# Two-step modulation blocks, more raw weight places and late matrix reads in a two-layer hybrid step

## The chip, the cores and the metric

The kernel runs on one core of a Trainium2 chip. The metric is the device time of one execution in microseconds (us), the median of several runs. One profiled execution of the kernel before is shown beside them; all rows of the trace are of that one.

## What is computed

The reference is one inference step of a hybrid backbone of two layers, in fp32. 128 prompt tokens and 256 sample tokens of width 1024 go through the same weights. Cut to what matters here:

```python
def layer(x, mod, p, lam_init, ctx, angs):
    sh1, sc1, g1, sh2, sc2, g2 = jnp.split(mod, N_MOD, axis=-1)
    h = rmsnorm(x, p['norm1_g']) * (1.0 + sc1) + sh1
    mix, st = token_mixers(h, p, lam_init, ctx, angs)   # four head groups, one of them an SSM
    x = x + g1 * mix
    h = rmsnorm(x, p['norm2_g']) * (1.0 + sc2) + sh2
    return x + g2 * sq_relu_mlp(h, p), st

def sq_relu_mlp(h, p):
    a = jax.nn.relu(h @ p['mlp_w1'])                    # 1024 x 4096
    return (a * a) @ p['mlp_w2']                        # 4096 x 1024

def adaln(cond, p):                                     # the modulation: 6 vectors of 1024
    return jax.nn.silu(cond) @ p['w_ada'] + p['b_ada']  # 1024 x 6144
```

The SSM part of `token_mixers` is not scanned step by step in the kernel: matrices that stand for the scan are built from its parameters and used in matmuls. One set of them is wanted for each layer.

## The kernel before

The 384 tokens are three tiles of 128. The work runs in five stages, which follow each other with some overlap: start, mix 0, MLP 0, mix 1, MLP 1. "mix" is normalization, the input projection, the four head groups and the output projection of a layer.

**Weights.** A matrix product in fp32 precision is made of three matmuls on a high and a low half of each operand (`mm3`). `stream` (line 833) fetches the weights in the order of a list: SP issues the DMA of one raw weight (512 KB) into a raw place ("wr"), ACT copies its high half and DVE subtracts the low half into a split place ("ws"), and the raw place is free again. Raw weights of the modulation (names ad1...) are not split: they stay in their raw place until PE has used them. `phase` (line 596) adds places to the base of three ws and four wr: in MLP 0 `CF["mlp"]` adds 3 ws, 4 small working tiles ("tk") and 2 wr.

**The MLP.** `mlp` (line 2223) walks through 16 pairs fp of two blocks i. `h1_block(fp, i)` makes 24 matmuls of 128x384 into a PSUM tile h with the two w1 halves of the pair (names w1, layer, pair, half: w10140 is layer 0, pair 14, half 0). ACT takes the relu to rl, DVE squares it, ACT copies the high half aT and DVE makes the low half. `w2_mm` then adds 18 matmuls of 128x512 into mo with one w2 weight per block (w2025 is layer 0, block 25). The h block of a pair stands one pair ahead of its mo.

**What else runs in MLP 0.** The modulation of layer 1 (`ada_split`, line 777) is done there, in 24 steps: three thirds of eight k. A step takes two raw weights (ad1hk0 and ad1hk1 for third h and step k) and is four column-tiled matmuls, which the trace shows as 8 records on 32 columns of the array; after each third come the transposes adat. `CF["adafp"]` says at which pairs steps are made, `CF["adan"]` how many behind each w2, `CF["adak"]` how many stand in one block. The SSM matrices of layer 1 are prepared there too (`ssm_tables`, and `ssm_ahead` with `ssm_prep`, on DVE and ACT in an area called arena): a quarter's matrices are written to DRAM by POOL (`WE<-arena`, 1.1 MB, four times) and its taps by ACT (`KD<-kb`). In mix 1 they are read back by `ssm_load` (line 1355) into tiles we and TT, by POOL's queue, two quarters at a time. The first two quarters' tiles have their room in MLP 0 already, so POOL issues those four reads in MLP 0.

**What sets the order.** Every operation is recorded by a helper (so all have line L366 in the trace), and a planner (`arrange`, line 423) orders each engine's operations by a due time to which the table `SHIFT` adds an offset for the kind of the tile that is written (`kind`, line 93: letters and one digit, mostly the layer). Manual dependencies then fix each engine's order. The engines and the DMA queues issue strictly in that order.

Of the kernel before, what the change touches and what calls it, by code (L numbers as in the profile page):

```python
# [20 lines left out]
L = 2  # L21
NT = 3

CF = {"order": "dba", "adafp": [2,3,4,5,6,7,8,9,10,11,12,13], "adan": 1, "psc": "VV", "qW": "Q", "adasplit": 0, "lq": 1, "KO": [3, 2, 1, 0], "adaat": 1, "kt": [["KTm", 1], ["QTm", 1], ["KTd", 1], ["QTd", 1]], "fair": 0, "adaf": 0, "eng": {"pT1": "A", "KTd": "A"}, "mlag": 4, "glag": 4, "NTK": 13, "W": 4, "prep": 0.0, "chain": 0.0, "tails": 0.0, "tailm": 0.0, "mla": 0.0, "gqa": 0.0, "diff": 0.0, "ada": 0.0,
      "stream": 0.0, "tab": 0.0, "main": 0.0, "tab1": 30.0, "rot": 10.0, "adak": 1, "balance": 0, "xbt": [2, 4], "xoff": 3.0, "woff": 5.0, "modoff": 0.0, "ahead": 0.0, "aheadoff": 0.0, "rotoff": [40.0, 0.0], "taboff": 10.0, "xlag": 5.0, "epool": 0, "lowp": [], "rotp": [], "hlp": [],"xat": 9, "st0": 20.0, "xs": 4, "mlp": [[3, 4, 2], [4, 4, 4]], "np": 2, "n1": 1, "tm": 1, "lnlag": 0.0, "dlag": 0.0, "hb1need": ["mla"], "dneed": ["mla"], "opneed": ["diff0"], "w1m": 1, "lnb": [400, 300, 0], "cache": 0.0}
CFS = [{**CF, **CF.get(f"L{l}", {})} for l in range(2)]
NTK = CF["NTK"]
KO = tuple(CF["KO"])
if CF["order"] == "dba":
# [9 lines left out]
WEIGH = (0,)  # L39

SHIFT = {
# [24 lines left out]
    "out_new_diff_k_dram": -75.4, "out_new_diff_v_dram": 130.1, "out_new_gqa_k_dram": -5.5,  # L66
    "out_new_gqa_v_dram": -67.1, "out_new_mla_ckv_dram": 55.9, "out_new_mla_krope_dram": -124.5,
    "out_new_ssm_im_dram": 170.2, "out_new_ssm_re_dram": -36.4, "out_y_prompt_dram": 17.1,
# [21 lines left out]
    "zred": 25.0,}  # L90


def kind(n):

    m = re.match(r"([A-Za-z_]+)(\d?)", n)
    return m[1] + m[2]


# [435 lines left out]
def hybrid_step(ctx: ExitStack, tc: tile.TileContext, I, O, plan=None):  # L534
# [29 lines left out]
    def lo(shape, name, tag=None, bufs=1, dt=F32):  # L564
        return alloc("lo", shape, name, tag, bufs, dt)
# [782 lines left out]
    def ssm_taps(l, qt, eng=None):  # L1348
        kd = KD[l][qt]
        TT = lo([128, 4, 128], f"TT{l}{qt}", "TT", 2)  # L1350
        (eng or DK).dma_start(TT, bass.AP(tensor=kd.tensor, offset=kd.offset,
                                ap=[[16, 8], [960, 16], [240, 4], [1, 128]]))
        return TT

    def ssm_load(l, qt, out):

        we = lo([128, 2176], f"we{l}{qt}", "we", 2)
        P.dma_start(we, WE[l][:, qt])
        W = [we[:, d * 576:(d + 1) * 576].rearrange("p (g j c) -> p g j c", g=4, j=9) for d in range(2)]
        out[qt] = (W, we[:, 1152:2176].rearrange("p (d g s) -> p d g s", d=2, g=4), ssm_taps(l, qt, P))  # L1360
        yield
# [930 lines left out]
            rl = tk([128, 384], f"rl{l}{fp}{i}")  # L2292
            act(rl, ps[:, 0:384], AF.Relu)
            tt(rl, rl, rl, OP.mult)
            act(aT_[:, i, 0], rl, AF.Copy)
            tt(aT_[:, i, 1], rl, aT_[:, i, 0].bitcast(F32), OP.subtract)
            done(rl, ps)
# [288 lines left out]
```

## Time and profile before

| | us |
|---|---|
| runs | 1084.15, 1086.51, 1090.27 |
| median | 1086.51 |
| profiled execution | 1094.41 |
| its span | 1092.6 |
| PE busy in the span | 1017.6 |
| DVE, ACT, POOL busy | 704.9, 489.7, 71.6 |
| start (0 to 62), mix 0 (62 to 276) | 62, 214 |
| MLP 0 (276 to 604) | 328 |
| mix 1 (604 to 808) | 204 |
| MLP 1 (808 to 1085) | 277 |

The stages are cut where the first or last matmul of their kind stands in the trace. 198.68 MB pass the DMA engines in the span, 182 GB/s in the mean. To read it: PE's share says which engine bounds the whole; a stage's table says where PE is not busy; the list of waits says for whom; the timeline of the engine that it waited for says what that engine was doing.

### The profile page before, as it was taken

The page shows a single profiled execution, that of the slowest core. Times are in us where ns is not written, and L with a number is a line of the kernel's source. Part 1 is how long each engine was busy: PE and PEld are TensorE (multiplying, and loading weights), DVE is VectorE, ACT ScalarE, POOL GpSimd, SP SyncE. Part 2 cuts the span into 40 slices and gives each one's busy share as a digit, 9 for nine tenths or more (in the row PEclk, how much of TensorE's full clock was granted, in tenths as well). Part 3 has the DMA queues.
Part 4 walks back from the last instruction along what each step waited for, and adds up shares of the span by engine and source line. Part 5 has one row for each costly group of instructions (what it writes and reads, how often), then busy time and mean ns, then how long its engine had stood idle before and what let it go on. Part 6 is the DMA issues. An engine that isn't in the chain of part 4 may idle for free. (4 is left out here: it accounts for less than half of the span.)

```text
span 1092.6 us, 16805 instructions
## 1 busy us (share of the span) xinstructions
PE 1017.6 (93%) x6156; PEld 814.9 (75%) x6156; DVE 704.9 (65%) x1706; ACT 489.7 (45%) x1056; POOL 71.6 (7%) x140
## 2 busy tenths in 40 slices
PE   6599989999899899999799999998989999999996
PEld 1476746657898678788678787676779999999995
DVE  8988987767798745644235767988685433444345
ACT  2653447754642334324233543588555333433332
POOL 0021200002000000000000012000200000000001
PEclk9899999999899999999899999998999999999999
DMA  9674584558447776788974446500673334444202
GB/s 362 227 272 140 176 263 167 172 178 279 153 142 254 273 260 209 241 280 280 292 243 155 134 134 194 174 16 21 223 259 97 123 125 138 135 154 149 83 20 77
DMA packets 103812, 198.68 MB, mean 182 GB/s; under 512 B 11937, under 2 KB 60577, under 8 KB 102449
## 3 DMA queue, kind: packets, MB, share of 16 engines
q1 hardware_dynamic: 86192, 164.76, 46.0%
q10 hardware_dynamic: 15232, 16.85, 4.9%
q0 software_dynamic: 2304, 16.00, 4.3%
q8 instruction: 48, 0.79, 0.3%
q14 instruction: 36, 0.29, 0.1%
HBM read 175.22 MB, written 19.07 MB: 178 GB/s over the span
## 5 line engine op out<-in xcount | busy, mean ns | idle before, releaser
L366 PE MATMUL mo<-w,aT 128*128 128x512 f32 x1152 | 347.3, 395 | 0.0
L366 PE MATMUL h<-HT,w 128*128 128x384 f32 x1344 | 315.4, 341 | 13.7 <-ACT rl L366 7.3
L366 PEld LDWEIGHTS h<-HT,w 128*128 128x128 f32 x1344 | 245.4, 190 | 26.7 <-ACT rl L366 8.4
L366 PEld LDWEIGHTS mo<-w,aT 128*128 128x128 f32 x1152 | 213.9, 188 | 47.2 <-issue 9.5
L366 DVE TENSOR_TENSOR rl<-rl 128x384 f32<-128x384 f32 (+1 forms) x62 | 35.2, 569 | 110.2 <-ACT rl L366 110.2
L366 ACT ACTIVATE rl<-h 128x384 f32<-128x384 f32 x56 | 27.2, 486 | 153.9 <-PE h L366 143.3
L366 PE MATMUL op<-wo,HT 128*128 128x512 f32 x288 | 74.6, 406 | 2.7 <-DVE rseb L366 1.5
L366 PEld LDWEIGHTS op<-wo,HT 128*128 128x128 f32 x288 | 52.8, 190 | 15.1 <-DVE wo L366 3.9
L366 PE MATMUL ada<-adaw,sil 128*2 128x512 f32 (+1 forms) x192 | 35.6, 612 | 12.8 <-DVE rsaa L366 8.4
L366 PE MATMUL h1t<-w,HT 128*128 128x256 f32 x288 | 40.2, 299 | 6.5 <-ACT HT L366 6.3
L366 PEld LDWEIGHTS h1t<-w,HT 128*128 128x128 f32 x288 | 37.9, 205 | 7.8 <-ACT HT L366 7.2
L366 ACT ACTIVATE aT<-rl 128x384 fp32r<-128x384 f32 x56 | 29.3, 523 | 31.0 <-DVE rl L366 31.0
L366 DVE TENSOR_TENSOR aT<-rl,aT 128x384 fp32r<-128x384 f32 x56 | 31.1, 555 | 17.7 <-ACT aT L366 17.7
L366 POOL TENSOR_TENSOR x<-x,res 128x512 f32<-128x512 f32 x10 | 14.7, 1488 | 367.0 <-DVE res L366 348.0
L366 ACT ACTIVATE pd<-sd,nmxd 128x384 f32<-128x384 f32 (+1 forms) x48 | 24.3, 514 | 7.3 <-DVE nmxd L366 5.3
L366 PEld LDWEIGHTS ada<-adaw,sil 128*2 128x2 f32 (+1 forms) x192 | 3.9, 87 | 31.5 <-DMA adaw<-in_w_ada_dram 18.5
L366 PE MATMUL ip0c<-wi0c,HT 128*128 128x512 f32 x72 | 19.8, 427 | 7.6 <-ACT HT L366 7.4
L366 DVE TENSOR_REDUCE nmxd<-sd 128x1 f32<-128x384 f32 (+1 forms) x40 | 20.5, 524 | 5.4 <-PE sd L366 5.1
L366 PEld LDWEIGHTS ip0c<-wi0c,HT 128*128 128x128 f32 x72 | 14.0, 202 | 11.7 <-ACT HT L366 8.3
L366 PE MATMUL ip1b<-wi1b,HT 128*128 128x512 f32 x72 | 21.3, 427 | 0.0
L366 PE MATMUL ip0b<-wi0b,HT 128*128 128x512 f32 x72 | 21.2, 424 | 0.0
L366 PE MATMUL ip1a<-wi1a,HT 128*128 128x512 f32 x72 | 20.7, 418 | 0.0
(824 smaller groups left out, 1883.9 us busy)
## 6 DMA issues: line engine op xcount, KB each, us to landing
adaw<-in_w_ada_dram SPq DMA_DIRECT2D x48, 512.0 KB, 5.1
x<-x SPq DMA_DIRECT2D x36, 256.0 KB, 2.6
S<-ph POOLq DMA_DIRECT2D x2, 2400.0 KB, 8.5
phr<-S ACTq DMA_DIRECT2D x8, 600.0 KB, 5.6
WE<-arena POOLq DMA_DIRECT2D x4, 1088.0 KB, 5.6
we<-WE POOLq DMA_DIRECT2D x4, 1088.0 KB, 10.2
gate<-gate ACTq DMA_DIRECT2D x16, 256.0 KB, 5.9
x<-in_x_sample_dram SPq DMA_DIRECT2D x8, 256.0 KB, 6.3
```

Source lines behind the costliest of these rows:

```text
L366: r_ = f(*args, **kw)
```

## The change

1. Two modulation steps stand in one block (`adak` 2), and a block is made behind both w2 weights of every second pair (3, 5, ..., 13) in place of one step behind each w2 of the pairs 2 to 13. The list of weights has four modulation weights behind each w2 of those pairs.
2. MLP 0 has 8 raw places in place of 6, 5 split places in place of 6, and one working tile less.
3. A one-column tile `late` is copied by POOL from rl of block (13,1) of layer 0. Before POOL issues a read of we or TT it copies `late` into the first column of the tile that is to be read into; the read overwrites it.
4. All offsets in `SHIFT` are new. `kind` first takes a suffix like `_1` off a name.

The diff, with two rows of the table:

```diff
-CF = {..., "adafp": [2,3,4,5,6,7,8,9,10,11,12,13], "adan": 1, ..., "adak": 1, ..., "mlp": [[3, 4, 2], [4, 4, 4]], ...}
+CF = {..., "adafp": [3,5,7,9,11,13], "adan": 2, ..., "adak": 2, ..., "mlp": [[2,3,4],[4,4,4]], ...}
 SHIFT = {
-    "E0": -16.3, "E2": -15.4, "ET0": -39.7, "HT": 0.8, "Hc0": -102.9, ...
+    "E0": -42.8, "E2": -24.7, "ET0": -55.7, "HT": -9.6, "Hc0": -136.1, ...
...
 def kind(n):
-    m = re.match(r"([A-Za-z_]+)(\d?)", n)
+    m = re.match(r"([A-Za-z_]+)(\d?)", re.sub(r"_\d+$", "", n))
     return m[1] + m[2]
...
     def ssm_taps(l, qt, eng=None):
         kd = KD[l][qt]
         TT = lo([128, 4, 128], f"TT{l}{qt}", "TT", 2)
+        if eng is not None:
+            P.tensor_copy(TT[:, 0, 0:1], lcs["late"])
         (eng or DK).dma_start(TT, ...)
...
     def ssm_load(l, qt, out):
         we = lo([128, 2176], f"we{l}{qt}", "we", 2)
+        P.tensor_copy(we[:, 0:1], lcs["late"])
         P.dma_start(we, WE[l][:, qt])
...
             rl = tk([128, 384], f"rl{l}{fp}{i}")
             act(rl, ps[:, 0:384], AF.Relu)
             tt(rl, rl, rl, OP.mult)
+            if l + 1 < L and (fp, i) == (13, 1):
+                lcs["late"] = ct([128, 1], "late")
+                P.tensor_copy(lcs["late"], rl[:, 0:1])
             act(aT_[:, i, 0], rl, AF.Copy)
```

**POOL's queue, from the last write of the SSM matrices to the end of MLP 0.** WE and KD are the matrices and taps in DRAM, we10 and TT10 the tiles of layer 1's quarter 0, x100 a residual. Before:

```order
L366 DMA WE_1_88<-arena1_4466 128x2176 x4
L366 DMA TT10_6540<-KD_10_93 128x4x128
L366 DMA TT11_6544<-KD_11_94 128x4x128
L366 DMA we10_6538<-WE_1_88 128x2176
L366 DMA we11_6542<-WE_1_88 128x2176
L366 TENSOR_TENSOR x100_6205<-x100_6205,res200_6209 128x512
```

and after:

```order
L366 DMA WE_1_88<-arena1_4379 128x2176 x4
L366 COPY late_5891<-rl0131_5888 128x1
L366 COPY TT10_6543<-late_5891 128x1
L366 COPY TT11_6549<-late_5891 128x1
L366 DMA TT10_6543<-KD_10_93 128x4x128
L366 DMA TT11_6549<-KD_11_94 128x4x128
L366 COPY we10_6540<-late_5891 128x1
L366 COPY we11_6546<-late_5891 128x1
L366 DMA we10_6540<-WE_1_88 128x2176
L366 DMA we11_6546<-WE_1_88 128x2176
L366 TENSOR_TENSOR x100_6201<-x100_6201,res200_6205 128x512
```

The four reads now stand behind a copy that waits for rl of block (13,1), and nothing else has moved past them.

**ACT's queue around block (13,0).** w10140<-w10140r is the copy of a weight's high half, rl0130 the relu of block (13,0), aT013 the high half of pair 13. Before:

```order
L366 ACTIVATE w2025_5773<-w2025r_5757 128x1024
L366 ACTIVATE w2024_5729<-w2024r_5691 128x1024
L366 ACTIVATE w10140_5846<-w10140r_5842 128x1024
L366 ACTIVATE rl0130_5831<-h10130_5805 128x384
L366 ACTIVATE aT013_5830<-rl0130_5831 128x384
```

and after:

```order
L366 ACTIVATE w2025_5809<-w2025r_5781 128x1024
L366 ACTIVATE aT012_5688<-rl0121_5753 128x384
L366 ACTIVATE w10140_5814<-w10140r_5807 128x1024
L366 ACTIVATE rl0130_5832<-h10130_5794 128x384
L366 ACTIVATE aT013_5831<-rl0130_5832 128x384
```

In both the copy of w10140 stands ahead of rl of block (13,0); after, w2024 is copied earlier.

**SP's queue in the last pairs of MLP 0.** Before:

```order
L366 DMA w2024r<-in_mlp_w_dram 128x1024
L366 DMA ad1240r<-in_w_ada_dram 128x1024
L366 DMA ad1241r<-in_w_ada_dram 128x1024
L366 DMA w2025r<-in_mlp_w_dram 128x1024
L366 DMA w10140r<-in_mlp_w_dram 128x4x256
L366 DMA w10141r<-in_mlp_w_dram 128x4x256
L366 DMA ad1251r<-in_w_ada_dram 128x1024
L366 DMA ad1250r<-in_w_ada_dram 128x1024
L366 DMA w2026r<-in_mlp_w_dram 128x1024
L366 DMA w2027r<-in_mlp_w_dram 128x1024
```

and after:

```order
L366 DMA w2024r<-in_mlp_w_dram 128x1024
L366 DMA w2025r<-in_mlp_w_dram 128x1024
L366 DMA w10140r<-in_mlp_w_dram 128x4x256
L366 DMA w2026r<-in_mlp_w_dram 128x1024
L366 DMA ad1241r<-in_w_ada_dram 128x1024
L366 DMA ad1250r<-in_w_ada_dram 128x1024
L366 DMA ad1251r<-in_w_ada_dram 128x1024
L366 DMA w10141r<-in_mlp_w_dram 128x4x256
L366 DMA ad1240r<-in_w_ada_dram 128x1024
L366 DMA w2027r<-in_mlp_w_dram 128x1024
```

w10140r now stands ahead of the modulation weights of steps 4 and 5, which come four together, and w10141r behind three of them.

## Rows read from the trace of the kernel before

**Rows 1.** The page: busy time, share of the span and instructions of each engine.

```profile
PE 1017.6 (93%) x6156; PEld 814.9 (75%) x6156; DVE 704.9 (65%) x1706; ACT 489.7 (45%) x1056; POOL 71.6 (7%) x140
```

**Rows 2.** Stretches, busy by engine, clock, DMA share, GB/s: MLP 0, MLP 1.

```profile
276.00:604.00 328.00, 310.16 (x1729) 260.00 (x1728) 193.35 (x406) 124.42 (x208) 11.04 (x20) 0.97 0.69 229
...
808.00:1085.00 277.00, 273.46 (x1421) 247.37 (x1420) 126.32 (x177) 103.24 (x156) 4.09 (x4) 0.99 0.36 112
```

**Rows 3.** Waits of PE in MLP 0: us in total, times, longest.

```profile
PE h L366 <- ACT rl L366: 7.3, 2, 6.7
PE h1t L366 <- ACT HT L366: 3.7, 1, 3.7
PE h L366 <- DVE w L366: 2.2, 1, 2.2
PE h L366 <- DVE kb L366: 2.2, 1, 2.2
PE h L366 <- ACT w L366: 2.1, 1, 2.1
```

**Rows 4.** Waits of PE in start and mix 0.

```profile
PE ip0c L366 <- ACT HT L366: 7.4, 2, 6.1
```

**Rows 5.** Short stretches of MLP 0, columns as in the second group.

```profile
371.36:374.77 3.41, 3.41 (x11) 3.41 (x12) 1.08 (x1) 0.00 (x0) 0.00 (x0) 0.50 0.99 348
...
519.00:546.00 27.00, 20.31 (x117) 17.87 (x110) 7.17 (x10) 6.36 (x10) 2.19 (x3) 0.87 0.98 295
542.13:545.43 3.30, 3.30 (x10) 3.30 (x11) 2.32 (x4) 1.47 (x2) 0.00 (x0) 0.50 0.64 184
573.00:604.00 31.00, 30.56 (x148) 25.94 (x146) 18.86 (x37) 12.33 (x25) 2.62 (x3) 1.00 0.47 156
```

**Rows 6.** Timeline of POOL, late MLP 0: start, duration, instruction, idle before.

```profile
516.11 0.53 POOL L366 DMA_DIRECT2D WE<-arena  x1 [39.78 <-ACT arena L366]
...
523.05 1.05 POOL L366 DMA_DIRECT2D TT<-KD  x1 [5.24 <-PE h L366]
524.09 1.15 POOL L366 DMA_DIRECT2D we<-WE  x2
```

**Rows 7.** Timelines of SP, ACT and PE around the longest wait of MLP 0.

```profile
523.25 0.38 SPq L366 DMA_DIRECT2D w10140r<-in_mlp_w_dram  x1
...
540.65 1.06 ACT L366 ACTIVATE w<-w10140r 128x1024 fp32r<-128x1024 f32 x1 [5.21 <-DMA w10140r<-in_mlp_w_dram]
541.61 0.47 ACT L366 ACTIVATE rl<-h 128x384 f32<-128x384 f32 x1
...
542.13 4.03 PE L366 MATMUL h<-HT,w 128*128 128x384 f32 x13 [6.69 <-ACT rl L366]
```

**Rows 8.** Timelines of SP and DVE around the waits at 368 to 372.

```profile
357.71 0.40 SPq L366 DMA_DIRECT2D w1060r<-in_mlp_w_dram  x1
...
371.22 1.21 DVE L366 TENSOR_TENSOR w<-w1061r,w 128x1024 fp32r<-128x1024 f32 x1
```

**Rows 9.** Timeline of PE: two modulation steps apart, and two together.

```profile
398.21 0.60 PE L366 MATMUL ada<-ad1060r,sil 128*2 128x512 f32 x2
...
399.07 0.62 PE L366 MATMUL pk<-arena 128*32 128x128 f32 x16
399.50 0.60 PE L366 MATMUL ada<-ad1070r,sil 128*2 128x512 f32 x2
...
400.48 0.51 PE L366 MATMUL mo<-w,aT 128*128 128x512 f32 x1
...
501.51 0.62 PE L366 MATMUL ada<-ad1200r,sil 128*32 128x512 f32 x2
...
503.36 3.69 PE L366 MATMUL mo<-w,aT 128*128 128x512 f32 x15
```

**Rows 10.** Timeline of PE: an undisturbed block of mo and of h.

```profile
381.87 4.26 PE L366 MATMUL mo<-w,aT 128*128 128x512 f32 x18
385.96 4.37 PE L366 MATMUL h<-HT,w 128*128 128x384 f32 x24
```

More of the change, by code (lines that the diff above doesn't have):

```diff
@@ L22 @@
 NT = 3
-CF = {"order": "dba", "adafp": [2,3,4,5,6,7,8,9,10,11,12,13], "adan": 1, "psc": "VV", "qW": "Q", "adasplit": 0, "lq": 1, "KO": [3, 2, 1, 0], "adaat": 1, "kt": [["KTm", 1], ["QTm", 1], ["KTd", 1], ["QTd", 1]], "fair": 0, "adaf": 0, "eng": {"pT1": "A", "KTd": "A"}, "mlag": 4, "glag": 4, "NTK": 13, "W": 4, "prep": 0.0, "chain": 0.0, "tails": 0.0, "tailm": 0.0, "mla": 0.0, "gqa": 0.0, "diff": 0.0, "ada": 0.0,
-      "stream": 0.0, "tab": 0.0, "main": 0.0, "tab1": 30.0, "rot": 10.0, "adak": 1, "balance": 0, "xbt": [2, 4], "xoff": 3.0, "woff": 5.0, "modoff": 0.0, "ahead": 0.0, "aheadoff": 0.0, "rotoff": [40.0, 0.0], "taboff": 10.0, "xlag": 5.0, "epool": 0, "lowp": [], "rotp": [], "hlp": [],"xat": 9, "st0": 20.0, "xs": 4, "mlp": [[3, 4, 2], [4, 4, 4]], "np": 2, "n1": 1, "tm": 1, "lnlag": 0.0, "dlag": 0.0, "hb1need": ["mla"], "dneed": ["mla"], "opneed": ["diff0"], "w1m": 1, "lnb": [400, 300, 0], "cache": 0.0}
+CF = {"order": "dba", "adafp": [3,5,7,9,11,13], "adan": 2, "psc": "VV", "qW": "Q", "adasplit": 0, "lq": 1, "KO": [3, 2, 1, 0], "adaat": 1, "kt": [["KTm", 1], ["QTm", 1], ["KTd", 1], ["QTd", 1]], "fair": 0, "adaf": 0, "eng": {"pT1": "A", "KTd": "A"}, "mlag": 4, "glag": 4, "NTK": 13, "W": 4, "prep": 0.0, "chain": 0.0, "tails": 0.0, "tailm": 0.0, "mla": 0.0, "gqa": 0.0, "diff": 0.0, "ada": 0.0,
+      "stream": 0.0, "tab": 0.0, "main": 0.0, "tab1": 30.0, "rot": 10.0, "adak": 2, "balance": 0, "xbt": [2, 4], "xoff": 3.0, "woff": 5.0, "modoff": 0.0, "ahead": 0.0, "aheadoff": 0.0, "rotoff": [40.0, 0.0], "taboff": 10.0, "xlag": 5.0, "epool": 0, "lowp": [], "rotp": [], "hlp": [],"xat": 9, "st0": 20.0, "xs": 4, "mlp": [[2,3,4],[4,4,4]], "np": 2, "n1": 1, "tm": 1, "lnlag": 0.0, "dlag": 0.0, "hb1need": ["mla"], "dneed": ["mla"], "opneed": ["diff0"], "w1m": 1, "lnb": [400, 300, 0], "cache": 0.0}
 CFS = [{**CF, **CF.get(f"L{l}", {})} for l in range(2)]
@@ L41 @@
 SHIFT = {
[24 rows of a table removed]
-    "out_new_diff_k_dram": -75.4, "out_new_diff_v_dram": 130.1, "out_new_gqa_k_dram": -5.5,
-    "out_new_gqa_v_dram": -67.1, "out_new_mla_ckv_dram": 55.9, "out_new_mla_krope_dram": -124.5,
-    "out_new_ssm_im_dram": 170.2, "out_new_ssm_re_dram": -36.4, "out_y_prompt_dram": 17.1,
[21 rows of a table removed]
-    "zred": 25.0,}
[25 rows of a table added]
+    "out_new_gqa_k_dram": -5.3, "out_new_gqa_v_dram": -105.9, "out_new_mla_ckv_dram": 93.3,
+    "out_new_mla_krope_dram": -199.6, "out_new_ssm_im_dram": 236.8, "out_new_ssm_re_dram": -3.6,
[22 rows of a table added]
 def kind(n):
-    m = re.match(r"([A-Za-z_]+)(\d?)", n)
+    m = re.match(r"([A-Za-z_]+)(\d?)", re.sub(r"_\d+$", "", n))
     return m[1] + m[2]
```

92 rows, old and new, of the table SHIFT are left out of this document.

## Prediction

> **What bounds the kernel now.** I read the page first: PE is busy 1017.6 us of a span of 1092.6 [rows 1]. So the matmuls are the bound, and a change that leaves their number and shape alone can only win back PE's idle time and the time in which PE runs at its lower clock. The second view is the table by stage. Layer 0's MLP lasts 328 us of the span with PE busy 310.16 and a mean granted clock of 0.97; the same MLP of layer 1, which carries no modulation and no SSM tables, has PE busy 273.46 of 277 us at 0.99 [rows 2]. The stage that the change works on is therefore the one with most to give. The third view lists who kept PE waiting in that stage: h waits 7.3 us for ACT's rl (6.69 of it at once, at 542.13), and once each for ACT's w (2.1), DVE's w (2.2) and DVE's kb (2.2); h1t waits 3.7 us for ACT's HT at the head of the stage [rows 3]. The fourth is the granted clock behind the waits: at 371.36 to 374.77 and at 542.13 to 545.43 PE runs at 0.50, which is 1.2 of 2.4 GHz, straight after it had been idle [rows 5]. At half clock a stretch costs half its length: 3.41 / 2 = 1.7 us and 3.30 / 2 = 1.65 us.
>
> So what can be won back in this stage, leaving the 3.7 us at its head (normalization, not touched), is 7.3 + 2.1 + 2.2 + 2.2 = 13.8 us idle, and 3.35 us of clock: **17.1 us** at most.
>
> **Why the waits are there.** The big one: from 516 to 525 us POOL puts the last write of the SSM matrices into DRAM (WE) and then reads blocks of them back: two TT, the later at 523.05, and two we at 524.09 [rows 6]. The raw weight w10140r is issued at 523.25, in the middle of that; ACT waits 5.21 us for it and copies it only at 540.65, and behind that copy in ACT's queue stands rl of block (13,0), which PE's next accumulation needs. PE starts again at 542.13 [rows 7]. In 519 to 546 us the DMA engines are 0.98 busy at 295 GB/s [rows 5]: the transfers are the limit, not the engines. The other one: the raw w1060r goes out only at 357.71, when modulation matmuls have given raw places back, and DVE, which has the SSM tables to do, splits w1061r at 371.22, and PE goes on at 371.36 [rows 5, 8].
>
> **The change part by part.**
>
> *Matrices return late.* In the order, POOL's four reads stand behind a copy from rl of block (13,1), and so go out when that block is done. By the order of the changed kernel, with the durations of [rows 10], some 23 us of matmul stand between that point and the first matmul on w10150, the first w1 weight that has to pass these reads, and some 14 us up to the modulation weights ad1270 and ad1271. The four reads are 2 x 1.09 + 2 x 0.26 = 2.7 MB, 9.2 us at the 295 GB/s of [rows 5]. With a copy and a split of about 1.1 and 1.2 us behind the landing, w10150 has room; ad1270 and ad1271, 1.05 MB, need 12.7 us if reads and weights all have to pass first, of 14. I therefore take away the 542 stall (6.69 + 1.65 = 8.3 us) and put 1.5 us back, between 0 and 6. The reads are used in mix 1 alone, after 604 us, and from 573 to 604 the DMA is 0.47 busy [rows 5], so they are not late for that. The new wait stands in POOL's queue: behind it are only those reads and the adds of the residual at the stage's end, and POOL is busy 7% of the span [rows 1], so the column copies cost nothing on the path. The two reads that belong to mix 1 itself pay only a column copy.
>
> *More raw places (6 to 8), fewer split places (6 to 5).* Modulation weights stay in their raw place until their matmul. With eight places a waiting block of two steps holds four and leaves four to the stream, where six left two. I take away the waits on w (2.1 + 2.2 + 0.6 = 4.9 us, the 0.6 being the small rest of rl's) with the clock behind them (1.7), 6.6 us, and put 1.0 back, 0 to 4, since a split place fewer must bite somewhere. The wait on kb (2.2 us) is one of the SSM preparation, which stands further ahead in the new order; I take half, 1.1 us, 0 to 2.2.
>
> *Blocks of two steps.* What a block costs on PE: two steps apart from each other take 399.07 - 398.21 = 0.86 and 400.48 - 399.50 = 0.98 us, together 1.84; two steps in one block take 503.36 - 501.51 = 1.85 us [rows 9]. So a step costs the same either way, if it has a neighbour of its own kind. In the order of before, seven of the blocks already stand in pairs and eight of the ten others share their excursion with pk; PE leaves its full array 13 times in this stage in the old order and 14 times in the new. The part itself: 0, within 0.5 us either way. Here a rule of the Trainium skill speaks for more than I give. TensorEngine Tiling (Array Packing), Key Properties, says that a change of tiling mode drains TensorE, so fewer, larger blocks ought to be cheaper; by a drain of 0.12 us (next paragraph's row) for 12 blocks instead of 24 that would be some 3 us more. The rows show that the pairs were mostly there already.
>
> *The new order.* Counted in the two orders, PE changes its array's tile 20 times more (mix 0 90 to 98, MLP 0 26 to 28, mix 1 65 to 75). A step that ends in pk keeps the narrow columns and takes 0.86 us, one that ends in mo 0.98 [rows 9]: 0.12 us a change, 20 x 0.12 = **2.4 us** lost, 0 to 2.6. The rest of the order in start, mix 0 and mix 1 I set at nothing, within 5 us either way: the largest wait there that an order can touch is ip0c's 7.4 us for ACT's HT [rows 4], ahead of which the new order puts the next tile's transposes, with HT's copy slightly later.
>
> **Sum** on the profiled execution (1094.4 us, span 1092.6): -8.3 + 1.5 - 6.6 + 1.0 - 1.1 + 2.4 = **-11.1 us**, so 1083.3. The median of the runs shown is 1086.5, 7.9 us below the profiled one; part of the profile's stalls may be its own, so I take off one us of the gain: **-10, 1076.5 us**, -0.9%. About 0.5% (5.4 us) is what a measurement of this kernel can tell from no change. With the bounds of the terms the forecast's own range is 1070 to 1081.
>
> **The rivals.**
>
> *A. The stall moves along.* The reads are the same 2.7 MB, and the stream around them is not lighter: behind block (13,1) four modulation weights, then w10150 to w2029. If the reads stretch those as they stretched w10140r, from 523.25 to 540.65 = 17 us [rows 7], ad1270 and ad1271 come 3 to 8 us too late, PE idles and drops to the lower clock, and 6.8 us of the gain are gone; with one more wait on a split place the rest goes too. -11.1 + 6.8 = -4.3, or + 5.6 = +1.3: 1082 to 1088, say 1085. For it: 17 us for 0.5 MB. Against it: the reads meet no WE write any more and half the weights of the last pairs, where the DMA falls to 0.47 [rows 5]. The Trainium skill's DMA: Bandwidth & Descriptors, Queues, rings and completion order, says that each DMA engine takes the queues that have work in turn; by that rule POOL's reads take their share from SP's weights wherever they are put, which is this rival. The rows of 519 to 546 us agree with it, and do not tell what happens with the WE write gone. I give it 0.21.
>
> *B. Slower: the loaded pairs starve.* A pair of blocks without modulation is 2 x 24 h and 2 x 18 mo matmuls. 18 mo take 385.96 - 381.87 = 4.09 us and 24 h at most 4.37 [rows 10], so 2 x 8.46 = 16.9 us. With four steps at 0.92 it is 20.6 us. In the loaded pair the stream wants 4 weights and 8 modulation weights of 0.52 MB, 6.3 MB, in these 20.6 us: 305 GB/s, above the 295 that the DMA gave when it was full [rows 5]. The order before spread the same bytes evenly (4.2 MB a pair). It decides on whether the free pair before, which wants 2.1 MB in 16.9 us, may run ahead: the loaded pair needs 0.2 MB in advance, and the free one has four raw places and five split places for it. If it may not, each of the six loaded pairs idles 6.3 MB at 295 GB/s = 21.3, less 20.6, so 0.7 us at least, and may pay 1.7 us of clock as at 371.36: 6 x 2.4 = 14.4 us. -11.1 + 14.4 = +3.3, and with the SSM writes in between (1.1 MB at 295 GB/s, 3.8 us, in two of the pairs) +11: 1090 to 1098, say 1094. For it: the 6.6 us that the one stall of this kind cost around 371.36 [rows 3, 5]. Against it: a lead of one weight does. I give it 0.18.
>
> *C. Everything comes back.* No residue, changes of tile free, some of ip0c's 7.4 us [rows 4] too: -17.1, 1067 to 1070. I give it 0.12.
>
> **How the numbers follow.** Forecast 0.49, A 0.21, B 0.18, C 0.12. Faster by over 0.5% (below 1081): the forecast nearly whole and C, with a little of A: 0.61. Within 0.5% (1081 to 1092): most of A and the edges of the forecast and B: 0.21. Slower: most of B, 0.18. The range, 1066 to 1091, leaves out B's greater part and the tail of C.
>
> **What would show it.** Right: PE without a wait over 2 us between 290 and 600 us, no stretch at 0.50 there, the stage some 12 us shorter, the first TT and we read some 10 to 15 us later than now, right behind block (13,1), ada records in blocks of 16 at 1.85 us. A: a wait on ada or h just after the reads go out, with ACT or PE waiting for ad1270, ad1271 or w10150. B: waits at ada or at w in several of the six pairs, each with a stretch at 0.50. Wrong in size: more idle PE in mix 0 or mix 1 than before.

## The result, and the profile after

| | before | after |
|---|---|---|
| median of the runs (six each) | 1090.55 us | 1078.58 us |
| lowest to highest | 1084.15 to 1092.95 | 1075.41 to 1080.28 |
| ratio | | 0.9897, 95% interval 0.9876 to 0.9919 |
| span of the profiled execution | 1092.6 us | 1077.7 us |

The changed kernel is 1.0% faster, 12 us; the forecast was 10 us less. Where the time went is read from stages cut at the same event in both traces: first matmul of the input projection (ip0c, ip1c), first matmul of the MLP (h1t).

| stage | before | after |
|---|---|---|
| to the first h1t of layer 0 | 279.94 | 277.29 |
| from there to the first ip1c (MLP 0) | 325.41 | 312.75 |
| to the first h1t of layer 1 (mix 1) | 205.44 | 205.37 |
| to the end | 281.84 | 282.34 |

So 12.7 of the 14.9 us by which the profiled span shrank lie in MLP 0. These rows are of one execution each: the profiled one of before (1094.41 us) lies 3.9 us above its median, that of after (1079.53) 1.0 above, so the medians bear out 12.0 of the 14.9 us. The page of after, with the line that answers to [rows 1]:

```profile
span 1077.7 us, 16837 instructions
...
PE 1015.3 (94%) x6156; PEld 812.6 (75%) x6156; DVE 701.2 (65%) x1706; ACT 486.2 (45%) x1056; POOL 72.7 (7%) x149
```

The waits of PE from 274 to 600 us of after, columns as in [rows 3]:

```profile
PE h L366 <- ACT rl L366: 3.9, 1, 3.9
PE htb L366 <- ACT xnb L366: 3.1, 1, 3.1
PE ip1c L366 <- ACT HT L366: 2.1, 2, 1.6
```

The four kinds of [rows 3] that made up 13.8 us within the MLP are down to one wait of 3.9 us; htb and ip1c stand at the stage's ends. That one wait, in the timelines of POOL, SP, ACT and PE of after:

```profile
532.19 0.19 POOL L366 COPY late<-rl 128x1 f32<-128x1 f32 x1 [52.92 <-DVE rl L366]
...
536.36 1.15 POOL L366 DMA_DIRECT2D we<-WE  x2 [0.18 <-POOL we L366]
...
535.89 0.38 SPq L366 DMA_DIRECT2D w10150r<-in_mlp_w_dram  x1
...
549.50 1.06 ACT L366 ACTIVATE w<-w10150r 128x1024 fp32r<-128x1024 f32 x1 [16.61 <-DMA w10150r<-in_mlp_w_dram]
550.46 0.47 ACT L366 ACTIVATE rl<-h 128x384 f32<-128x384 f32 x1
...
550.98 5.24 PE L366 MATMUL h<-HT,w 128*128 128x384 f32 x20 [3.91 <-ACT rl L366]
```

It is the picture of [rows 7], one pair later: the reads go out, the first w1 weight among them (issued 535.89, half a us ahead of the two large ones) is copied 13.6 us later, rl stands behind that copy in ACT's queue, and PE waits for rl. Two stretches of after, columns as in [rows 5], show the DMA while that happens and the clock afterwards:

```profile
550.98:554.20 3.22, 3.22 (x10) 3.22 (x11) 2.24 (x4) 1.47 (x2) 0.00 (x0) 0.50 0.77 216
535.00:552.00 17.00, 13.09 (x77) 9.03 (x70) 1.41 (x2) 1.44 (x2) 2.33 (x5) 0.96 0.98 309
```

The DMA is 0.98 busy, and PE runs at 0.50 for 3.22 us behind the wait. 3.91 + 3.22 / 2 = 5.5 us stand there in place of the 8.3 us of before.

### The profile page after: what moved, and what is told of

It is laid out like the page before. It is cut to its first block, busy times and chain, and to the rows that moved or that the text cites. A ratio compares the mean times of both kernels' runs of the same rounds, so it can differ in the third digit from the quotient of the medians.

```text
span 1077.7 us, 16837 instructions
## 1 busy us (share of the span) xinstructions
PE 1015.3 (94%) x6156; PEld 812.6 (75%) x6156; DVE 701.2 (65%) x1706; ACT 486.2 (45%) x1056; POOL 72.7 (7%) x149
## 5 line engine op out<-in xcount | busy, mean ns | idle before, releaser
L366 PE MATMUL mo<-w,aT 128*128 128x512 f32 x1152 | 311.9, 395 | 0.0
L366 PE MATMUL h<-HT,w 128*128 128x384 f32 x1344 | 279.8, 340 | 3.9 <-ACT rl L366 3.9
L366 PEld LDWEIGHTS h<-HT,w 128*128 128x128 f32 x1344 | 240.4, 189 | 19.2 <-ACT rl L366 5.2
L366 PEld LDWEIGHTS op<-wo,HT 128*128 128x128 f32 x288 | 52.5, 188 | 16.2 <-DVE wo L366 4.0
L366 PE MATMUL ada<-adaw,sil 128*2 128x512 f32 (+1 forms) x192 | 35.1, 610 | 13.8 <-DMA adaw<-in_w_ada_dram 13.6
L366 PE MATMUL ip0a<-wi0a,HT 128*128 128x512 f32 x72 | 21.6, 420 | 0.2 <-DVE t1a L366 0.2
L366 PE MATMUL ip1c<-wi1c,HT 128*128 128x512 f32 x72 | 19.0, 417 | 2.2 <-ACT HT L366 2.1
```

Of the source, the lines that this page charges most:

```text
L366: r_ = f(*args, **kw)
```

## The experiments

Each ratio is against the kernel before on the same chip, with its 95% interval in brackets. Differences in us between two changed kernels are of medians that were taken in part on different chips (the medians of before itself lie up to 3 us apart), so verdicts go by the ratios. The first question was whether the late reads are what helped. Four kernels move the reads alone.

**Late reads alone.** The kernel before, with

```diff
+            if l + 1 < L and (fp, i) == (13, 1):
+                lcs["late"] = ct([128, 1], "late")
+                P.tensor_copy(lcs["late"], rl[:, 0:1])
...
+            P.tensor_copy(TT[:, 0, 0:1], lcs["late"])
...
+        P.tensor_copy(we[:, 0:1], lcs["late"])
```

> The kernel before with the third part of the change alone: the four matrix reads stand behind a copy from rl of block (13,1); the rest of the order is the same but for a few rows. Theory (the reads are the cause of the 542 us stall, and half of the gain is theirs): the wait of 6.69 us at 542 and its stretch at half clock go, 8.3 us; behind block (13,1) a residue like that of the changed kernel comes (3.9 us idle and 1.7 us of clock), so 3 to 8 us less than before, ratio 0.993 to 0.997. The waits at 368 to 378 and at 403 us stay. Rival (the new order alone made the gain): the stall only moves some 10 us later at its full size, ratio 0.998 to 1.002.

Measured: 1089.16 us, ratio 1.0003 (0.9977 to 1.0029). Nothing is won. Timelines of SP, ACT and PE of that kernel:

```profile
542.52 0.38 SPq L366 DMA_DIRECT2D w10150r<-in_mlp_w_dram  x1
...
558.71 1.06 ACT L366 ACTIVATE w<-w10150r 128x1024 fp32r<-128x1024 f32 x1 [11.96 <-DMA w10150r<-in_mlp_w_dram]
...
560.20 3.25 PE L366 MATMUL h<-HT,w 128*128 128x384 f32 x9 [6.29 <-ACT rl L366]
```

The wait of 6.69 us at 542 is gone and one of 6.29 us stands at 560, with w10150 (16.2 us to its copy) in the place of w10140. The rival held: the stall moves along at its size.

**The change without late reads.** The changed kernel with the lines of the diff above taken out:

> The changed kernel without its late reads: the four reads go out right behind the last write of the SSM matrices, which ends some 485 us into the span now. Theory: the reads then meet the stream of a loaded pair, a stall of 4 to 8 us stands at 490 to 505 us, and the 3.9 us at 551 with its clock (5.6 us together) goes: 0 to +3 us against the changed kernel. Rival (with the last write 30 us earlier and eight raw places the reads do no harm anywhere): 5 us faster than the changed kernel, ratio to before about 0.985. Rival (late reads are the whole gain): 8 us slower than the changed kernel or more.

Measured: 1069.06 us, ratio 0.9812 (0.9794 to 0.9829): about 9 us faster than the changed kernel, and the fastest so far. The theory fell; its first rival held and gave even more. Of the 10.9 us between the two profiled spans (1077.7 and 1066.8) 6.5 lie in MLP 0; 2.4 lie ahead of its first h1t, where the reads have not gone out yet, and are not shown to be theirs. From the first h1t (274.92) to the first ip1c (581.17) PE now waits 0.5 us in sum ahead of ip1c; the stage is 306.25 us long. The reads have gone back to their old place in the order, right behind the last write. POOL's and SP's timelines there, with two stretches around it and the copy of the next w1 weight on ACT:

```profile
475.45 0.53 POOL L366 DMA_DIRECT2D WE<-arena  x1 [30.20 <-ACT arena L366]
...
487.77 1.15 POOL L366 DMA_DIRECT2D we<-WE  x2
...
479.29 0.33 SPq L366 DMA_DIRECT2D ad1220r<-in_w_ada_dram  x1
487.19 0.33 SPq L366 DMA_DIRECT2D x<-x  x1
487.70 0.33 SPq L366 DMA_DIRECT2D ad1221r<-in_w_ada_dram  x1
490.96 0.33 SPq L366 DMA_DIRECT2D ad1230r<-in_w_ada_dram  x1
493.45 0.33 SPq L366 DMA_DIRECT2D ad1231r<-in_w_ada_dram  x1
...
495.12 0.38 SPq L366 DMA_DIRECT2D w10130r<-in_mlp_w_dram  x1
...
504.80 1.06 ACT L366 ACTIVATE w<-w10130r 128x1024 fp32r<-128x1024 f32 x1 [2.58 <-DMA w10130r<-in_mlp_w_dram]
...
510.97 0.49 ACT L366 ACTIVATE rl<-h 128x384 f32<-128x384 f32 x1 [0.88 <-PE h L366]
```

```profile
470.00:500.00 30.00, 30.00 (x177) 25.23 (x176) 11.17 (x16) 9.50 (x16) 3.82 (x5) 1.00 0.98 340
475.00:503.00 28.00, 28.00 (x162) 23.36 (x162) 8.81 (x14) 7.65 (x13) 3.82 (x5) 1.00 0.98 336
```

The DMA is as full as at 519 to 546 before (0.98), and PE is busy all of the 28 us. What meets the reads here are four modulation weights, whose matmul comes at 504.43, and no weight that ACT has to copy ahead of an rl: SP issues none from 475 to 495. w10130r, issued behind them at 495.12, still takes 9.7 us to its copy, and ACT waits 2.58 us for it; it does no harm, since the next rl in ACT's queue stands at 510.97.

**The reads one block later.** The changed kernel with one line changed; in the order only POOL's queue differs:

```diff
-            if l + 1 < L and (fp, i) == (13, 1):
+            if l + 1 < L and (fp, i) == (14, 1):
```

> The changed kernel with the reads one block later, behind rl of block (14,1); nothing else in the order moves. Theory (the 3.9 us at 551 come from the reads meeting w10150, which landed 13.6 us after its issue): the wait is gone or under 1 us, no stretch at half clock at 551, 4 to 6 us less than the changed kernel, about 1073 to 1075 us. Rival (the wait comes from the burst of five weights that go out within 4 us there): w10150 still takes over 9 us, the wait stays at 2 us or more, 0 to 2 us gained.

Measured: 1070.93 us, ratio 0.9831 (0.9816 to 0.9847). PE's wait at 551 is gone, as expected, and MLP 0 is 307.4 us long. The gain on the changed kernel, some 7 us, is more than the 4 to 6 expected. SP and ACT in that kernel:

```profile
533.59 0.38 SPq L366 DMA_DIRECT2D w10150r<-in_mlp_w_dram  x1
...
538.65 1.06 ACT L366 ACTIVATE w<-w10150r 128x1024 fp32r<-128x1024 f32 x1 [8.06 <-DMA w10150r<-in_mlp_w_dram]
```

The same weight goes out in the same burst of five and is copied 5.1 us after its issue, not 13.6. So the burst is not the cause, the reads are.

**The reads one block later in the kernel before.** As the first, with (14, 1):

> The kernel before with the four reads behind rl of block (14,1); nothing else moves but a few rows. Theory (the reads cost what the next w1 weights lose, and after block (14,1) no w1 weight is left to be slowed): the 6.7 us wait at 542 goes and none comes at 560, 8 us less than before, ratio 0.991 to 0.994, with the waits of 2 us at 368, 371 and 403 us still there. Rival (the stall at 542 is the last SSM write meeting the loaded stream, and the reads only add to it): a wait of 3 us or more stays at 540, ratio over 0.996.

In the trace the theory holds: no wait at 542 and none at 560, and MLP 0 is 318.2 us long, 7.2 less; the waits of 2.6, 1.5 and 1.8 us at 368, 370 and 401 stay. SP and ACT of that kernel, whose last write (514.33) still stands some 7 us ahead of w10140r:

```profile
521.02 0.38 SPq L366 DMA_DIRECT2D w10140r<-in_mlp_w_dram  x1
...
528.35 1.05 ACT L366 ACTIVATE w<-w10140r 128x1024 fp32r<-128x1024 f32 x1
530.95 0.49 ACT L366 ACTIVATE rl<-h 128x384 f32<-128x384 f32 x1 [1.56 <-PE h L366]
```

With the write in its place and the reads away, w10140r takes 7.3 us to its copy, without a wait of ACT, where it took 17.4 [rows 7]. So in these two executions it was the reads, and not the write, that made the stall at 542. In time it is 1085.05 us, ratio 0.9982 (0.9961 to 1.0002), 2 to 3 us and not 8. The profiled execution of before (1094.4 us) lies above all its timed runs on every chip (at most 1093.67), and its stall may be larger than theirs; why the timed gain is so much smaller stays open.

The second question was which of the other parts carries the gain. Each of the new offsets, the blocks of two and the places (eight raw and five split, one tile less) was taken alone and in pairs, all with the reads right behind the last write.

**New offsets alone.** The kernel before with the new table, and the suffix taken off the names:

```diff
 SHIFT = {
-    "E0": -16.3, "E2": -15.4, ...
+    "E0": -42.8, "E2": -24.7, ...
...
```

> The kernel before with the new offsets alone (and the suffix taken off the names): single steps, six raw and six split places, reads right behind the last SSM write. Theory (the new offsets carry the gain, by taking the SSM preparation some 30 us ahead, so that the last write and the reads no longer meet w10140): MLP 0 has under 4 us of waits, ratio 0.982 to 0.988. Rival (the blocks of two and the eight raw places carry it, and the offsets only fit them): waits of 8 us or more stay in MLP 0, ratio 0.995 or more.

Measured: 1094.07 us, ratio 1.0065 (1.0034 to 1.0096): slower. Waits of PE in MLP 0:

```profile
PE h L366 <- ACT w L366: 6.2, 2, 4.1
PE ada L366 <- DMA ad1260r<-in_w_ada_dram: 3.7, 1, 3.7
PE mo L366 <- ACT w L366: 3.2, 1, 3.2
```

My theory for this run fell: the offsets do not carry the gain by themselves.

**Blocks and places with the old offsets.** The changed kernel without late reads and with the table of before:

> The changed kernel without its late reads and with the offsets of before: blocks of two, eight raw and five split places. Theory (the new offsets carry the gain): waits of 8 us or more in MLP 0, the total 8 us or more above the changed kernel without late reads (1069 us), ratio 0.990 to 1.000. Rival (places and blocks carry it): within 3 us of that kernel, ratio 0.981 to 0.985.

Measured: 1085.13 us, ratio 0.9982 (0.9956 to 1.0007), 16 us above the same kernel with the new offsets (18 by the ratios): the theory held for this pair of kernels. Its longest wait, in the timelines of SP, ACT and PE:

```profile
488.88 0.38 SPq L366 DMA_DIRECT2D w10121r<-in_mlp_w_dram  x1
...
507.42 1.06 ACT L366 ACTIVATE w<-w10121r 128x1024 fp32r<-128x1024 f32 x1 [6.44 <-DMA ad1200r<-in_w_ada_dram]
...
508.53 0.62 PE L366 MATMUL h<-HT,w 128*128 128x384 f32 x2 [3.53 <-ACT w L366]
```

Here too the reads go out at 487.88 to 488.91, but the old offsets have a w1 weight, w10121, at 488.88, which takes 18.5 us to its copy (the profile puts the end of ACT's wait down to ad1200r, issued behind it on SP's queue at 492.15). Here PE waits for that copy itself, and not for an rl behind it.

**The places of before in the changed kernel**, again without late reads:

```diff
-"mlp": [[2,3,4],[4,4,4]]
+"mlp": [[3,4,2],[4,4,4]]
```

> The changed kernel without its late reads and with the places of before: six raw, six split, one working tile more. Theory (a waiting block of two holds four raw places, and two left are too few): PE waits at ada or at w in several of the six loaded pairs, 4 to 12 us more than the changed kernel without late reads, ratio 0.985 to 0.993. Rival (the places do not matter): within 2 us of it, ratio 0.980 to 0.983.

Measured: 1077.32 us, ratio 0.9917 (0.9885 to 0.9948), 8 us more than with the new places (11 by the ratios): in the expected range, but with one wait, not several:

```profile
363.07 1.20 PE L366 MATMUL mo<-w,aT 128*128 128x512 f32 x2 [4.86 <-ACT w L366]
```

**Single steps in the changed kernel**, first with the late reads, then without:

```diff
-"adafp": [3,5,7,9,11,13], "adan": 2, ... "adak": 2
+"adafp": [2,3,4,5,6,7,8,9,10,11,12,13], "adan": 1, ... "adak": 1
```

> The changed kernel with the modulation as before: one step behind each w2 of the pairs 2 to 13, one step in a block; places, late reads and offsets as changed. Theory (blocks of two cost PE what two steps cost): MLP 0's PE busy time within 1 us; the total within 3 us of the changed kernel either way, by what the order makes of it. Rival (every leaving of the full array costs a drain): 12 more excursions, 3 us slower and PE busy 2 to 3 us more in MLP 0.

Measured with late reads: 1076.13 us, ratio 0.9882 (0.9860 to 0.9904), not to be told from the changed kernel (0.9876 to 0.9919). PE is busy 1014.8 us in the span, against 1015.3. No cost of smaller blocks shows, but the premise of twelve more excursions was wrong as well: the planner put neighbours together, and PE leaves its full array 13 times, against 14. In this order w10150r goes out at 535.15, ahead of the reads at 537.83, and is copied at 539.52; there is no wait at 551.

> The changed kernel without its late reads and with single steps as before: eight raw and five split places, new offsets. Theory (the two extra raw places are most of what makes the new offsets pay, the blocks bring the SSM preparation ahead): the last SSM write stands near 500 us, as in the run with single steps and late reads, the reads meet the stream of the pairs behind it, a wait of 2 to 5 us at 515 to 530; 1072 to 1077 us, ratio 0.985 to 0.990. Rival (blocks are what matters, not places): 1085 us or more. Rival (places alone matter): 1067 to 1070 us.

Measured without: 1081.76 us, ratio 0.9940 (0.9918 to 0.9962), between the theory's range and the rival's. The last write stands at 501.82 and the wait at 515.01 is 2.53 us, as expected; the whole is 5 to 10 us more than I had put it. With single steps the late reads thus gain some 6 us (0.9882 against 0.9940), where with blocks of two they cost 9: what they are worth hangs on what else stands in the queues. SP and ACT of the two kernels, with late reads and then without:

```profile
497.06 0.38 SPq L366 DMA_DIRECT2D w10130r<-in_mlp_w_dram  x1
...
505.70 1.06 ACT L366 ACTIVATE w<-w10130r 128x1024 fp32r<-128x1024 f32 x1 [3.49 <-DMA w10130r<-in_mlp_w_dram]
```

```profile
497.74 0.38 SPq L366 DMA_DIRECT2D w10130r<-in_mlp_w_dram  x1
...
513.52 1.06 ACT L366 ACTIVATE w<-w10130r 128x1024 fp32r<-128x1024 f32 x1 [10.63 <-DMA w10130r<-in_mlp_w_dram]
514.49 0.47 ACT L366 ACTIVATE rl<-h 128x384 f32<-128x384 f32 x1
```

Both have the last write some 4 us behind w10130r, at 501.14 and 501.82. Without late reads POOL also issues the first read of TT (256 KB) at 502.42, and the copy comes 15.8 us after the issue and not 8.6. The two large reads go out only at 512.45.

**The new places alone**, in the kernel before:

> The kernel before with the places of the changed one alone: eight raw, five split, one working tile less; single steps, old offsets, reads right behind the last SSM write. Theory (the waits on w at 368 to 378 us come from too few raw places): these are gone, the stall at 542 stays at 5 to 8 us, 3 to 6 us less than before, ratio 0.994 to 0.997. Rival (one split place less costs what two raw places give): ratio 0.998 to 1.003, with waits on w elsewhere.

Measured: 1093.52 us, ratio 1.0051 (1.0029 to 1.0073): slower, on neither side. The waits on w at 368 to 378 are gone, as the theory said (0.4 us at most is left there), but ACT waits for w2025, which was issued right behind the large reads of 511.30, 14.9 us earlier, and PE waits for w10131, whose copy stands behind it:

```profile
513.30 0.33 SPq L366 DMA_DIRECT2D w2025r<-in_mlp_w_dram  x1
...
528.18 1.06 ACT L366 ACTIVATE w<-w2025r 128x1024 fp32r<-128x1024 f32 x1 [9.71 <-DMA w2025r<-in_mlp_w_dram]
...
530.65 1.01 PE L366 MATMUL h<-HT,w 128*128 128x384 f32 x2 [7.13 <-ACT w L366]
```

**The blocks alone**, in the kernel before, with six raw places:

> The blocks of two at every second pair alone: six raw and six split places, old offsets, reads right behind the last SSM write. Theory (a waiting block of two holds four of six raw places, and with offsets that were not made for it the stream starves): PE waits of 10 us or more in MLP 0 at w or ada, slower than before, ratio 1.000 to 1.010. Rival (the blocks alone take the SSM writes ahead and out of the way of w10140): the stall at 542 is gone, ratio 0.990 to 0.996.

Measured: 1104.06 us, ratio 1.0165 (1.0136 to 1.0194): the slowest, by the mechanism expected and beyond the range expected (1.000 to 1.010). Waits of PE in its MLP 0:

```profile
PE h L366 <- ACT w L366: 7.8, 4, 3.2
PE mo L366 <- ACT w L366: 3.7, 1, 3.7
PE h L366 <- DVE kb L366: 3.2, 2, 2.8
```

**One working tile more** in the kernel without late reads (`"mlp": [[2,4,4],...`):

> The changed kernel without its late reads and with one working tile more in MLP 0 (17 as before, not 16). Theory (the second block of transposes at the head of MLP 0 waits 3 us for ACT's xnb because a working tile is short; the run with six raw places and 17 tiles has its first h1t 3.4 us earlier): the head wait of 3.1 us goes and MLP 0 keeps its 0.5 us of waits, 2 to 4 us less than without, about 1066 us, ratio 0.977 to 0.980. Rival (the head is set by the order, not by the tile): within 1 us of it, 1069 us.

Measured: 1068.58 us, ratio 0.9831 (0.9810 to 0.9852). The rival held: the wait for xnb stays at 3.05 us, and the time cannot be told from that of the kernel with 16 tiles.

All the kernels with the reads right behind the last write, in one table. "Last write" is the start of POOL's last WE<-arena and in brackets its distance from the first h1t; the waits are PE's of 1 us or more between that h1t and the transposes hta at the end of MLP 0.

| offsets | blocks of | raw places | ratio | MLP 0, us | last write | waits |
|---|---|---|---|---|---|---|
| old | 1 | 6 | 1 | 325.4 | 516 (236) | 2.1, 2.2, 2.2, 6.7 |
| old | 1 | 8 | 1.0051 | 327.8 | 501 (221) | 1.2, 7.1 |
| old | 2 | 6 | 1.0165 | 340.1 | 489 (213) | 1.1, 3.7, 2.8, 1.9, 3.1, 3.2 |
| old | 2 | 8 | 0.9982 | 317.5 | 476 (198) | 2.0, 1.2, 3.5 |
| new | 1 | 6 | 1.0065 | 335.9 | 523 (252) | 1.5, 4.1, 3.2, 2.1, 3.7 |
| new | 1 | 8 | 0.9940 | 317.6 | 502 (225) | 1.3, 2.5 |
| new | 2 | 6 | 0.9917 | 316.1 | 480 (209) | 4.9 |
| new | 2 | 8 | 0.9812 | 306.3 | 475 (201) | none |

Each of these three parts alone makes the kernel slower by 0.5 to 1.7%. Together they make it 1.9% faster. Places bring the last write 15 us ahead, blocks 23, both 38 (old offsets, in brackets); the offsets put it 3 to 16 us later in three of the four pairs and 4 ahead in one (blocks of two, six places).

## Why the prediction was right, and where it was not

**What bounds the kernel: right.** The gain lies in MLP 0, in waits and in stretches at half clock. The kernel without late reads has none of either within the stage (from 281 to 575 us PE is busy all of the 294 us, at 1.00), which shows that the 17.1 us could be had in full, as in rival C: MLP 0 went from 325.4 to 306.3 us, 19.1.

**The sum: right in size by luck, wrong in its terms.** MLP 0 was to give -8.3 + 1.5 - 6.6 + 1.0 - 1.1 = -13.5 us and gave -12.7. But the end stall gave -8.3 + 5.5 = -2.8, where I had put -6.8: the residue was 5.5 and not 1.5, within its bounds of 0 to 6 and near the worst. The waits on w and on kb, with their clock, gave -6.6 - 2.2 = -8.8, where I had put -6.7: nothing came back for the missing split place, and the whole wait on kb went. The two errors of 4.0 and 2.1 us stand against each other; the last us or so is in part the half clock at the stage's head, which reaches 6 us beyond the first h1t before (to 286) and 4 after (to 281). On the profiled executions the whole was put at -11.1 us and came to -14.9: MLP 0 gave 0.8 less than put, and the rest of the program, put at +2.4, gave -2.2. The upper end of my own range was wrong as well: with the bounds that I had set for the terms the sum runs from -17.1 to -2.3, which is 1070 to 1085 and not 1081.

**Late reads: the step that failed.** I took the stall at 542 for the reads' work and the late reads for its cure. The first holds (with the reads behind block (14,1) of the kernel before, w10140r takes 7.3 us and not 17.4); the second is wrong at the place that the change gives them. Late reads alone gave nothing (1.0003), and in the changed kernel they cost about 9 us (0.9897 with them, 0.9812 without), 6.5 of them seen in MLP 0. What takes the stall away is that the reads do not meet a weight that ACT copies right ahead of an rl: in the kernel without late reads they go out from 476 to 488, where there is none, and behind block (14,1) no w1 weight is left; behind block (13,1) there is w10150. My working had the 23 us between the reads and w10150's first matmul, and missed what [rows 7] show: it is not that matmul which waits. ACT takes the copy of w10150 in its turn, at 549.50, long before the matmul, which by the order of the h blocks comes at 560.98, and the rl of block (14,0) is behind it. The time to count was from the weight's issue to the next rl in ACT's queue.

**Rival A** described what happened at that place. Its sign came, and mine, no wait over 2 us and no stretch at 0.50, did not: PE waits 3.91 us at 551, behind ACT's wait for w10150. Of A's price of 6.8 us 4.0 were paid. 0.5 MB took 13.6 us to its copy where it took 5.1 without the reads. The rule of the Trainium skill's DMA: Bandwidth & Descriptors, Queues, rings and completion order, that each DMA engine takes the queues with work in turn, agrees with these two numbers; but the same full DMA did no harm at 475 to 503, so where a share is taken matters, not that it is.

**Raw places and blocks.** That more raw places end the waits on w at 368 to 378 holds: with the places alone they are gone. My reading of those waits named the wrong weight, though. SP and DVE of before:

```profile
359.97 0.37 SPq L366 DMA_DIRECT2D w1050r<-in_mlp_w_dram  x1
...
370.09 1.22 DVE L366 TENSOR_TENSOR w<-w1050r,w 128x1024 fp32r<-128x1024 f32 x1
371.22 1.21 DVE L366 TENSOR_TENSOR w<-w1061r,w 128x1024 fp32r<-128x1024 f32 x1
```

PE goes on at 371.36 when the split of w1050r is done (371.31), not that of w1061r (372.43), and w1050r was issued behind both halves of pair 6. From 340 to 360 SP waited 7.4 us for DVE's splits, 7.7 for transfers and 0.5 for modulation matmuls, so it was not mainly the modulation that held the stream up there. That a block of two needs them holds too: 1.0165 with six, 0.9982 with eight places under the old offsets. I had not seen that each part alone loses. Rival B's starving loaded pairs are what the blocks alone show; with eight places and fitting offsets they do not come.

**Blocks cost PE nothing: not contradicted.** With single steps PE's busy time is the same within 0.5 us. As the planner joined the singles, no run here shows what the drain in the Trainium skill's TensorEngine Tiling (Array Packing), Key Properties, would cost over twelve more excursions.

**The new order.** The 2.4 us that I set for twenty more changes of tile do not show: mix 1, with ten of them, has 205.37 against 205.44 us. Whether they are hidden or cheaper was not tried. That the rest of the order is worth nothing within 5 us held (-2.65 ahead of MLP 0, 0.4 after it), but the offsets are worth 16 us of the whole (18 by the ratios), 11 of them in MLP 0, given blocks and places, and cost 6.5 us without them.

The best kernel found is the changed one without its late reads, 0.9812 of before. With one working tile more, or with the reads behind block (14,1), it is at 0.9831, too near to be told apart.

## What to carry to other kernels

A transfer that may run early is best put where the weights that it delays have no reader in a busy in-order queue; look for what stands behind the delayed weight's first consumer, and not only for when the weight is multiplied (in two of the kernels PE waited for the weight itself). Offsets, buffer counts and the grouping of work fit each other: test a part in the setting that it was made for and also alone, and take each part of a joint change out once, since one of them may cost what the others gain. The late reads gained 6 us, gave nothing or cost 9 us by what stood around them.

## What the hardware showed that was not expected

A full DMA is not one rate. The engines were 0.98 busy at 295 GB/s in 519 to 546 us before, at 309 in 535 to 552 after, and at 340 in 470 to 500 without late reads. With single steps and late reads the share is full at 388 GB/s:

```profile
497.00:513.50 16.50, 16.50 (x103) 13.68 (x102) 5.51 (x10) 6.51 (x11) 0.53 (x1) 1.00 1.02 388
```

I had used 295 as the ceiling for rival B's 305 GB/s; it was none.

What a read cost a weight did not go by its bytes. With the one TT read of 256 KB under way w10130r took 15.8 us to its copy, and 8.6 without it, where 256 KB at 295 GB/s would be 0.9 us (an estimate). This is one pair of executions; what it is about this read was not tried.

A wait of some 2 us does not always bring the half clock. Behind the waits at 368 and 371, together 4.3 us, PE ran at 0.50 [rows 5]; behind the 2.17 us at 403 (the kb of [rows 3]) the clock stayed at 1.00. At the same matmul of the kernel with late reads alone 2.24 us were followed by 0.51 (401.1 to 404.5), and behind the 3.53 us at 508.53 with blocks, places and the old offsets it stayed at 1.00 (508.5 to 511.9). So the same wait can cost some 1.7 us more in one execution than in another.
